# Softmax division moved from VectorE to ScalarE in two attentions

## The chip, the cores and the metric

The kernel runs on one core of one Trainium2 chip. The metric is the device time of one execution in microseconds. The kernel before takes 1680.43 us, the median of three runs (1677.56 to 1681.21 us).

## The reference, cut to what matters

A first model of two layers (gated linear attention, an mLSTM, a mixture of experts after each) is followed by a second one of two layers, called l0 and l1 here. Only the attentions of the second are touched. Each of its layers has two of them, over 256 tokens, with heads of 64 columns:

```python
s = jnp.einsum('bqgrd,bkgd->bgrqk', qi, k) * scale      # attention A: 8 query heads, 2 key heads
p = jax.nn.softmax(s, axis=-1)
o = jnp.einsum('bgrqk,bkgd->bqgrd', p, v)
# attention B: three dilated groups for each of 4 heads; their three softmaxes are
# joined by softmax(lse), which is one softmax over the keys of all three groups
```

A softmax is computed as the row's maximum, the exponential of the shifted scores with the row's sum, the reciprocal of the sum, and a product of each row with its reciprocal. That product is what moves.

In each layer a conditioning vector c also makes six columns of shifts, scales and gates, `silu(c) @ w_ada + b_ada`, from 24 MB of weights. The text calls this the ada work.

## The kernel before, in words

The five engines run their own instruction lists in order and wait for each other by semaphores. The lists are written by a Python program that calls every operation once, in program order, so the list of an engine is the order of the calls. All calls go through a wrapper (`Timed`, L165), so the profile has L175 for nearly every instruction; rows are told apart by their tiles.

**The dense stream.** The kernel multiplies in fp32 by splitting every weight w into hi (ScalarE cast, 128x1024) and lo (VectorE, w minus hi), with three matmuls each (X_H with hi, X_H with lo, X_L with hi). Weights come in units of 1 MB through the SP queue; `Stream.split` (L351) makes hi and lo two chunks ahead of their use. If hi is late, lo is late, because lo reads hi.

**Background work.** Attention, norms and ada work are Python generators, advanced by `B.tick()` after each small group of dense matmuls. So their instructions stand between those of the dense stream, on each engine.

**Two attentions in a layer.** `attend_a` (L2168) runs in four instances, two at a time: scores `sa` (PSUM bank group `acc`, four banks), `softmax` (L2140), transposes of the result `pa` into `pta`, a copy to `pTa`, and the product `oa`. A round is two instances at once: two maxima `mx`, eight exponentials of 128x256, two reciprocals `smx`, eight divisions. While a round runs, its scores hold all four acc banks until the exponentials have read them. The transposes `rtp` of the next queries and keys need such banks. `attend_b` (L2198) runs in four instances as well, with 128x512 tiles `pb`, four exponentials and four divisions in a round.

**What sets the order.** The program keeps a clock of its own (`Clock`, L107, with costs in `Timed.cost`, L187): an estimate of when each engine is through. Three kinds of decisions hang on it. `AV` (L235) puts a copy on ScalarE or VectorE, whichever it expects to be done first; `VG2` does so for VectorE and GpSimd. `calm` (L1950) holds back an ada step while ScalarE or VectorE is expected to run over 0.9 us behind TensorE, for up to ten ticks. `Hooks` (L556) releases the small `part` with `fold` matmuls when both engines are expected to have caught up. So an operation that changes its engine moves others.

**The ada work** (`ada_cols`, L1854) goes in pieces of 512 KB through a ring of two tiles `ada_w`. A piece is a DMA, a ScalarE copy with a scale for each partition into `ada_t`, a VectorE scalar_tensor_tensor that adds its second half, and from the second piece on an addition. Four pieces make a group, which ends in a transpose, a reduction into `part`, and the fold on TensorE. The load of the next piece but one is issued when a piece's VectorE step has read its tile. A layer must have ten groups before its second norm: `emit` (L2306) in the output projection calls `ada_need(l, 9)` (L1957), which issues the remaining pieces with no dense matmuls between them.

Of the kernel before, what the change touches and what calls it, by code (L numbers as in the profile page):

```python
# [30 lines left out]
AF = mybir.ActivationFunctionType  # L31
OP = mybir.AluOpType
# [195 lines left out]
def tile_model(ctx: ExitStack, tc: tile.TileContext, I, out, stages=None, h_in=None):  # L228
    nc = tc.nc
    clock = Clock()  # L230
    PE, V, A, G = [Timed(clock, e, n) for e, n in
                   ((nc.tensor, "PE"), (nc.vector, "V"), (nc.scalar, "A"), (nc.gpsimd, "G"))]
# [1788 lines left out]
    def attention(l, x, at):  # L2021
# [118 lines left out]
        def softmax(pss, held, ps_, ng):  # L2140

            mx = small.tile([P, 2, ng], F32, name="mx", tag="mx", bufs=4)
            for i in range(2):
                V.tensor_reduce(mx[:, i], pss[i], axis=AX.X, op=OP.max)
            V.tensor_scalar(mx, mx, -0.125, None, op0=OP.mult)
            yield 1
            sm = small.tile([P, 2, ng], F32, name="smx", tag="smx", bufs=4)
            for i in range(2):
                for j in range(ng):
                    A.activation(ps_[i][:, j], pss[i][:, j], AF.Exp, bias=mx[:, i, j:j + 1], scale=0.125,  # L2150
                                 accum_out=sm[:, i, j:j + 1])
            for b in held:
                b[0] = True
            yield 1
            V.reciprocal(sm, sm)
            for i in range(2):
                for j in range(ng):
                    V.tensor_scalar(ps_[i][:, j], ps_[i][:, j], sm[:, i, j:j + 1], None, op0=OP.mult)
            yield 1

        oaT = (at.tile([P, 4, T], F32R, name="oaTh"), at.tile([P, 4, T], F32R, name="oaTl"))
# [6 lines left out]
        def attend_a(j):  # L2168
            yield from wait_for(0, 1)
            yield  # L2170
            yield from room(2)
            pss = [acc_ps((P, 2, T), name="sa", read=False) for _ in range(2)]
            held = banks[-2:]
            for mt in range(2):
                for r in range(2):
                    s = slice(r * 64, r * 64 + 64)
                    PE.matmul(pss[r][:, mt], qaT[s, j, mt * P:(mt + 1) * P], kaT[s, 0], start=True, stop=True)
            yield
            pp = [at.tile([P, 2, T], F32, name="pa", tag="p", bufs=4) for _ in range(2)]
            yield from softmax(pss, held, pp, 2)  # L2180
            pT = at.tile([P, 2, 2, T], F32, name="pTa", tag="pT", bufs=2)
            for r in range(2):
                yield from room(1)
                tp = acc_ps((P, 2, 2, P), name="pta")
                for kt in range(2):
                    for mt in range(2):
                        PE.transpose(tp[:, kt, mt], pp[r][:, mt, kt * P:(kt + 1) * P], c_ident)
                AV.copy(pT[:, r], tp.rearrange("p k m q -> p k (m q)"))
                yield
            yield from room(1)  # L2190
            o = acc_ps((P, T), name="oa")
            for kt in range(2):
                for r in range(2):
                    PE.matmul(o[r * 64:r * 64 + 64], va[:, kt, r * 64:r * 64 + 64], pT[:, r, kt],
                              start=kt == 0, stop=kt == 1)
            put_o((oaT[0][:, j], oaT[1][:, j]), o)

        def attend_b(j, mt):  # L2198
# [16 lines left out]
            yield  # L2215
            pp = [at.tile([P, 1, 512], F32, name="pb", tag="p", bufs=4) for _ in range(2)]
            yield from softmax(pss, held, pp, 1)
            pT = at.tile([P, 2, 4, P], F32, name="pTb", tag="pT", bufs=2)
            for r in range(2):
# [450 lines left out]
```

## Time and profile before

| what | number |
|---|---|
| median of three runs | 1680.43 us |
| the profiled execution's own time | 1678.68 us |
| its span (first to last instruction) | 1676.6 us |
| TensorE busy | 1552.8 us |
| VectorE busy | 954.2 us |
| ScalarE busy | 699.6 us |
| attention of l0 in the span | about 884 to 1008 us |
| attention of l1 in the span | about 1306 to 1428 us |
| mean granted TensorE clock | 0.97 |

In the profile PE is TensorE, DVE is VectorE, ACT is ScalarE, POOL is GpSimd and SP is the queue that issues the loads. A row of a timeline has the start in us, the length in us of the instruction or of several alike, the engine, the operation, the tile written and the tiles read, the shape, a count, and in brackets the idle time of the engine just before and what released it.

### The profile page before, as it was taken

To read this page: it belongs to the slowest core of one execution; us is meant where nothing else is said; L and a number is where in the kernel's file an instruction comes from. 1 tells how busy PE (TensorE), PEld (TensorE's weight loads), DVE (VectorE), ACT (ScalarE), POOL (GpSimd) and SP (SyncE) were. 2 spreads that over 40 slices of the span, in tenths; PEclk is the share of its full clock that TensorE was granted. 3 is DMA by queue.
4 is the path that set the end of the run, shared out by engine and by line. 5 is a ranking of instruction groups with operands and counts; after the bars stand their busy time and mean duration, and the time that the engine had idled before them with its cause. 6 is when DMAs were issued, how large, how long until landed. Compare 5 with 4: busy or idle time off the path is not lost. (4 is left out here: it accounts for less than half of the span.)

```text
span 1676.6 us, 22592 instructions
## 1 busy us (share of the span) xinstructions
PE 1552.8 (93%) x8773; PEld 1118.0 (67%) x8774; DVE 954.2 (57%) x1640; ACT 699.6 (42%) x1130; POOL 200.0 (12%) x187
## 2 busy tenths in 40 slices
PE   7998999898899989998889998699998999999996
PEld 5865444336776644443367897589986779879995
DVE  3676113106787531111288868777779976875543
ACT  5533111104544221111155654566565555465552
POOL 1010000001333100000142100200015310020000
PEclk9999999999999999999999999899999999999999
DMA  9847999999765399999854666588875446746551
GB/s 320 302 157 258 351 401 411 393 383 210 254 202 218 119 339 360 406 404 386 300 201 139 201 177 236 155 276 287 286 264 172 151 159 171 237 164 225 177 175 50
DMA packets 165771, 422.44 MB, mean 252 GB/s; under 512 B 13017, under 2 KB 14193, under 8 KB 154642
## 3 DMA queue, kind: packets, MB, share of 16 engines
q1 hardware_dynamic: 165458, 420.75, 72.1%
q8 instruction: 73, 1.20, 0.3%
q14 instruction: 48, 0.39, 0.1%
q0 software_dynamic: 192, 0.10, 0.0%
HBM read 419.77 MB, written 1.05 MB: 251 GB/s over the span
## 5 line engine op out<-in xcount | busy, mean ns | idle before, releaser
L175 DVE TENSOR_TENSOR lo<-w,hi 128x1024 fp32r<-128x1024 f32 x282 | 346.4, 1238 | 131.3 <-ACT hi L175 130.9
L175 ACT CAST hi<-w 128x1024 fp32r<-128x1024 f32 x301 | 310.0, 1051 | 99.8 <-PE mm L175 69.7
L175 PE MATMUL mm<-hi,X_H 128*128 128x512 f32 x512 | 216.2, 422 | 16.2 <-ACT X_H L175 8.5
L175 PE MATMUL mm<-lo,X_H 128*128 128x512 f32 x512 | 207.0, 404 | 3.2 <-DVE lo L175 2.9
L175 PE MATMUL mm<-X_H,hi 128*128 128x256 f32 x704 | 202.8, 288 | 0.0
L175 PE MATMUL mm<-X_L,hi 128*128 128x256 f32 x704 | 199.0, 283 | 0.0
L175 PE MATMUL mm<-X_H,lo 128*128 128x256 f32 x704 | 199.0, 283 | 0.0
L175 PE MATMUL mm<-hi,X_L 128*128 128x512 f32 x512 | 192.8, 399 | 2.5 <-DVE X_L L175 2.4
L175 PE MATMUL up<-w,X 128*64 128x512 f32 x672 | 193.7, 597 | 0.6 <-ACT X L175 0.6
L175 PEld LDWEIGHTS mm<-X_H,hi 128*128 128x128 f32 x704 | 134.5, 191 | 1.7 <-issue 0.7
L175 PEld LDWEIGHTS mm<-X_L,hi 128*128 128x128 f32 x704 | 134.7, 191 | 0.4
L175 PEld LDWEIGHTS mm<-X_H,lo 128*128 128x128 f32 x704 | 134.6, 191 | 0.0
L175 PEld LDWEIGHTS mm<-hi,X_H 128*128 128x128 f32 x512 | 99.3, 194 | 48.6 <-issue 14.1
L175 PEld LDWEIGHTS up<-w,X 128*64 128x64 f32 x672 | 58.6, 137 | 96.4 <-issue 92.8
L175 PEld LDWEIGHTS mm<-lo,X_H 128*128 128x128 f32 x512 | 99.7, 195 | 25.3 <-DVE lo L175 6.6
L175 PEld LDWEIGHTS mm<-hi,X_L 128*128 128x128 f32 x512 | 97.8, 192 | 27.1 <-DVE X_L L175 5.6
L175 PE MATMUL up<-wh,X 128*64 128x512 f32 x336 | 115.9, 601 | 0.0
L175 DVE SCALAR_TENSOR_TENSOR y<-dn,gsl,y 128x512 fp32r<-128x512 f32 x32 | 24.0, 750 | 158.5 <-ACT y L175 158.5
L175 PE MATMUL dn<-w,hTt 128*64 128x512 f32 x336 | 102.8, 614 | 2.1 <-ACT hTt L175 2.1
L175 PE MATMUL acc<-lo,fh 128*128 128x512 f32 x256 | 100.7, 393 | 0.3 <-DVE lo L175 0.3
L175 PE MATMUL acc<-hi,fl 128*128 128x512 f32 x256 | 100.8, 394 | 0.0
L175 PE MATMUL acc<-hi,fh 128*128 128x512 f32 x256 | 99.6, 389 | 0.0
(412 smaller groups left out, 2524.1 us busy)
## 6 DMA issues: line engine op xcount, KB each, us to landing
w<-in_moe_w SPq DMA_DIRECT2D x126, 1024.0 KB, 11.2
w<-in_w_ff SPq DMA_DIRECT2D x64, 1024.0 KB, 5.6
wh<-in_moe_w SPq DMA_DIRECT2D x124, 512.0 KB, 11.5
ada_w<-in_w_ada SPq DMA_DIRECT2D x96, 512.0 KB, 4.9
w<-in_w_in SPq DMA_DIRECT2D x40, 1024.0 KB, 5.4
w<-in_mlstm_w_in SPq DMA_DIRECT2D x16, 1024.0 KB, 19.3
w<-in_gla_w_in SPq DMA_DIRECT2D x12, 1024.0 KB, 9.8
w<-in_w_out SPq DMA_DIRECT2D x8, 1024.0 KB, 5.1
```

Of the source, the lines that this page charges most:

```text
L175: r = f(*args, **kw)
```

## The change

The division of each row of exponentials by its sum is an activation Copy on ScalarE with a scale for each partition, in place of a tensor_scalar on VectorE. The operands and the places of the calls are the same. Over the two layers these are 32 instructions on 128x256 and 16 on 128x512.

```diff
             V.reciprocal(sm, sm)
             for i in range(2):
                 for j in range(ng):
-                    V.tensor_scalar(ps_[i][:, j], ps_[i][:, j], sm[:, i, j:j + 1], None, op0=OP.mult)
+                    A.activation(ps_[i][:, j], ps_[i][:, j], AF.Copy, scale=sm[:, i, j:j + 1])
             yield 1
```

The order of other instructions moves with it. On ScalarE, in the first round of attention A in l0 (hi is the split of a weight, kbT a transposed key, sq a square for a norm, raw a sum of the ada work):

```order
 L175 CAST hi<-w 128x1024
 L175 COPY kbT_11584<-rtp 128x2x128
-L175 COPY raw<-mm 128x4
+L175 ACTIVATE pa<-pa,smx 128x256 x8
 L175 CAST hi<-w 128x1024
 L175 COPY kbT_11584<-rtp 128x2x128
 L175 ACTIVATE sq<-mm 128x256 x2
-L175 COPY pTa<-pta 128x512 x4
+L175 COPY pTa<-pta 128x512 x3
```

The eight divisions now stand ahead of the next hi, and one of the four copies pTa has gone to VectorE. The fold whose sum raw was copied here comes later.

On VectorE, just ahead of the maxima of the second round in l0 (xs, ro and rt are the rotary embedding, ada_t the ada work):

```order
 L175 TENSOR_TENSOR rt<-xs,cs 128x4x32
 L175 TENSOR_TENSOR xs<-ro,rt 128x256
+L175 SCALAR_TENSOR_TENSOR ada_t<-ada_w,ccol,ada_t 128x512
 L175 TENSOR_REDUCE mx<-sa 128x2 x2
 L175 TENSOR_SCALAR mx<-mx 128x4
```

An ada step that stood in the first round, behind the divisions, is now ahead of these maxima. The same move is in l1.

On VectorE, at the end of l0's output projection, around the two residual sums that `emit` makes for the first 128 tokens (res, h):

```order
 L175 TENSOR_TENSOR res<-mm,gt 128x512
 L175 TENSOR_TENSOR h<-h,res 128x512
-L175 STREAM_TRANSPOSE ada_t<-ada_t 128x512
-L175 TENSOR_REDUCE part<-ada_t 128x16
+L175 SCALAR_TENSOR_TENSOR ada_t<-ada_w,ccol,ada_t 128x512
+L175 TENSOR_TENSOR ada_t<-ada_t 128x512
 L175 TENSOR_TENSOR res<-mm,gt 128x512
 L175 TENSOR_TENSOR h<-h,res 128x512
-L175 COPY raw<-bgp 128x4
+L175 SCALAR_TENSOR_TENSOR ada_t<-ada_w,ccol,ada_t 128x512
+L175 TENSOR_TENSOR ada_t<-ada_t 128x512
+L175 STREAM_TRANSPOSE ada_t<-ada_t 128x512
```

At this point the ada work is two pieces further back than it was: they stood in the attention before. On the SP queue the run of ada loads at this place has eight in a row where it had six. Behind it the lists of all engines are the same again until the attention of l1.

## Rows read from the trace of the kernel before

**Rows 1.** The page: span, and busy time by engine.
```profile
span 1676.6 us, 22592 instructions
PE 1552.8 (93%) x8773; PEld 1118.0 (67%) x8774; DVE 954.2 (57%) x1640; ACT 699.6 (42%) x1130; POOL 200.0 (12%) x187
```
**Rows 2.** Busy time by stretch; PEclk is TensorE's granted clock.
```profile
890.00:910.00 20.00, 18.77 (x104) 13.86 (x105) 16.96 (x39) 13.98 (x34) 6.45 (x8) 1.00 0.50 160
910.00:930.00 20.00, 18.10 (x89) 13.16 (x86) 17.14 (x43) 11.39 (x33) 3.73 (x4) 0.91 0.41 131
970.00:990.00 20.00, 20.00 (x166) 18.03 (x165) 11.77 (x18) 11.35 (x22) 0.00 (x0) 1.00 0.73 171
1043.00:1058.00 15.00, 1.83 (x22) 1.23 (x21) 9.73 (x18) 4.41 (x10) 0.00 (x0) 0.65 0.70 228
```
**Rows 3.** Timeline of PE: matmuls behind idle time.
```profile
905.32 0.81 PE L175 MATMUL pta<-ident,pa 128*128 128x128 f32 x4 [0.45 <-DVE pa L175]
...
922.94 0.44 PE L175 MATMUL rtp<-ident,xs 128*128 128x128 f32 x2 [0.72 <-ACT pa L175]
...
1057.35 0.29 PE L175 MATMUL bgp<-part,fold 128*32 128x4 f32 x8 [12.21 <-DVE part L175]
...
1343.56 0.44 PE L175 MATMUL rtp<-ident,xs 128*128 128x128 f32 x2 [1.79 <-ACT pa L175]
```
**Rows 4.** By tile: count, then shortest, median and longest in ns.
```profile
L175 DVE TENSOR_SCALAR pa<-pa,smx x32: 341/348/372, 903.6 to 1354.3; 128x256 f32<-128x256 f32 x32
...
L175 DVE TENSOR_SCALAR pb<-pb,smx x16: 479/484/489, 967.6 to 1421.3; 128x512 f32<-128x512 f32 x16
...
L175 ACT ACTIVATE ada_t<-ada_w,ccol x96: 706/722/770, 57.6 to 1561.6; 128x512 f32<-128x512 f32 x96
```
**Rows 5.** Timeline of ACT, first round of attention A in l0.
```profile
901.18 1.08 ACT L175 CAST hi<-w 128x1024 fp32r<-128x1024 f32 x1
902.12 0.42 ACT L175 COPY kbT<-rtp 128x256 f32<-128x256 f32 x1
...
904.14 0.67 ACT L175 ACTIVATE sq<-mm 128x256 f32<-128x256 f32 x2
...
907.99 1.07 ACT L175 COPY pTa<-pta 128x512 f32<-128x512 f32 x2 [1.23 <-PE pta L175]
908.95 1.06 ACT L175 CAST hi<-w 128x1024 fp32r<-128x1024 f32 x1
...
911.96 0.73 ACT L175 ACTIVATE ada_t<-ada_w,ccol 128x512 f32<-128x512 f32 x1
...
921.86 0.47 ACT L175 ACTIVATE pa<-sa,mx 128x256 f32<-128x256 f32 x1 [7.29 <-DVE mx L175]
```
**Rows 6.** Timeline of DVE, from the first round to the second's maxima.
```profile
903.64 1.14 DVE L175 TENSOR_SCALAR pa<-pa,smx 128x256 f32<-128x256 f32 x4
...
908.15 0.75 DVE L175 SCALAR_TENSOR_TENSOR ada_t<-ada_w,ccol,ada_t 128x512 f32<-128x512 f32 x1
910.04 1.23 DVE L175 TENSOR_TENSOR lo<-w,hi 128x1024 fp32r<-128x1024 f32 x1 [1.14 <-ACT hi L175]
...
920.28 1.28 DVE L175 TENSOR_REDUCE mx<-sa 128x2 f32<-128x512 f32 x2
```
**Rows 7.** Timeline of DVE, end of the output projection of l0.
```profile
1043.41 0.70 DVE L175 STREAM_TRANSPOSE ada_t<-ada_t 128x512 f32<-128x512 f32 x1
...
1047.56 1.42 DVE L175 SCALAR_TENSOR_TENSOR ada_t<-ada_w,ccol,ada_t 128x512 f32<-128x512 f32 x2 [1.13 <-ACT ada_t L175]
...
1052.96 0.75 DVE L175 SCALAR_TENSOR_TENSOR ada_t<-ada_w,ccol,ada_t 128x512 f32<-128x512 f32 x1 [3.26 <-ACT ada_t L175]
...
1054.35 0.75 DVE L175 SCALAR_TENSOR_TENSOR ada_t<-ada_w,ccol,ada_t 128x512 f32<-128x512 f32 x1
```
**Rows 8.** Timeline of ACT, the same place.
```profile
1046.82 1.32 ACT L175 ACTIVATE ada_t<-ada_w,ccol 128x512 f32<-128x512 f32 x2
1052.21 0.72 ACT L175 ACTIVATE ada_t<-ada_w,ccol 128x512 f32<-128x512 f32 x1 [4.07 <-DMA ada_w<-in_w_ada]
```

## The prediction

> **What bounds the kernel now.** I read the page first: TensorE (PE) is busy for 1552.8 of 1676.6 us, VectorE (DVE) for 954.2 and ScalarE (ACT) for 699.6 [rows 1]. So an engine that loses or gains work counts only where PE waits for it, and the average shares say nothing on that. The second view was the busy time by stretch. In attention B PE is busy for 20.00 of 20 us while DVE has 11.77 and ACT 11.35; in attention A PE idles for 1.23 us of one stretch and 1.90 of the next, with the granted clock at 0.91 in the latter; at the end of l0's output projection PE works for 1.83 of 15 us, at a clock of 0.65 [rows 2]. The third was PE's timeline with the brackets that name the releaser: in attention A it waits 0.45 us for the divided `pa`, and then for the exponentials of the next round, 0.72 us in l0 and 1.79 in l1, since the `rtp` transposes need a score bank that those have still to read; at the end of the projection it waits 12.21 us for `part` of the ada work [rows 3]. The tiles gave durations, the timelines of ACT and DVE what stands before each wait.
>
> **Price of the instruction.** On DVE a 128x256 division lasts 348 ns and a 128x512 one 484 [rows 4]. Four in a row take 1.14 us [rows 6], so they start (1.14 - 0.35)/3 = 0.26 apart; for the large ones I take 0.48 less the same overlap of 0.09, 0.40. DVE loses 32 x 0.26 + 16 x 0.40 = about 15 us of queue, ACT gets the same work at its own price. No row shows a 128x256 ACT copy with a scale for each partition. From below: two `sq` of that size, without such a scale, take 0.67 together, 0.28 apart if each lasts 0.39. From above: the 128x256 exponential lasts 0.47 [rows 5], with no overlap 0.5. The nearest row is the same operation at 512 columns, `ada_t`, 0.72 long [rows 4], two in 1.32 [rows 8], 0.60 apart. Two `pTa` of 512 columns take 1.07 [rows 5], 0.48 apart if one lasts 0.59; against `sq` 256 columns less are worth 0.20. I take 0.60 - 0.20 = 0.40 apart: eight take 3.2 us on ACT, 2.4 on DVE with the reciprocal between them.
>
> The Trainium skill prices this too. Its page "ScalarE: Activation LUTs" (section "What ACT_TABLE_LOAD costs") gives 186 ns, 0.833 ns a column, 93 ns for each pointer operand and 93 ns of overlap back to back. That is an estimate of 0.49 us long and 0.40 apart here; at 512 columns it is 0.71, where the trace has 0.72, so the trace agrees and the sum would be the same. The page's section "Rules for kernel authors" says that a multiplication belongs on VectorE and not on ScalarE, which speaks against the change; by the traces so far the larger price bears it out only where ACT is on the chain.
>
> **First round of attention A in l0.** On ACT the divisions come ahead of the next `hi` and of `sq`, `pTa` (order above), and they can't start before the reciprocals, which DVE does just ahead of 903.64 [rows 6]. ACT was through with that round's exponentials by 901.18, then did a `hi` and `kbT` [rows 5]; the other `hi`, which started at about 902.4, now stands behind eight divisions. They run from about 903.7 to 906.9. Behind them come that `hi` with 0.95, `kbT` 0.27, two `sq` 0.55 and three `pTa` about 1.5 (0.48 apart): the `hi` that started at 908.95 [rows 5] starts at about 910.2, 1.2 late. Its `lo`, which DVE began at 910.04 after an idle 1.14 us for `hi` [rows 6], begins at 911.2. DVE works from that `lo` to the maxima at 920.28 [rows 6] almost without a gap, so these are 1.2 late. The ada step that ran at 908.15 in idle time for 0.75 [rows 6] is now in this stretch ahead of the maxima (order above): 0.66 more. The exponentials start at 921.86 after ACT had idled 7.29 us for the maxima [rows 5]; they now start 1.9 later, and PE's `rtp` with them. PE itself gets the transposes of `pa` some 0.9 us later than at 905.32 [rows 3], which is ahead of the same wait and is swallowed by it. l1 shows the same wait for exponentials at 1343.56 [rows 3] and the same moves: 1.9 again.
>
> **Second rounds and attention B.** In the second round of A PE needs six of the eight divided tiles; the dearer ACT price and the copies ahead of them make these 0.3 us late in l0 and, as two copies more stand ahead there, 0.5 in l1. Attention A: 2.2 + 2.4 = 4.6. In attention B 4 x (0.60 - 0.40) = 0.8 us a round is hidden by PE, which has no idle time there while ACT has 8.65 of 20 free [rows 2]: cost 0. Without that cover a round costs up to 4 x 0.60 = 2.4.
>
> **The ada work at the end of l0.** What the attention has not done of it `emit` forces, with no matmuls between. By the order two pieces more are left: eight loads where there were six. Before, two pieces were added at 1047.56, then DVE idled 3.26 us until 1052.96 for a pair whose second step was at 1054.35 [rows 7]; ACT had idled 4.07 for the load [rows 8], whose tile came free only with the first pair. Then the fold ran at 1057.35 [rows 3]. So pair follows pair by 1052.96 - 1047.56 = 5.4 us: add, load, scale. A pair more costs at most that, and at least two DVE steps, 1.4 (two in 1.42 [rows 7]), if its data lies ready. Worked through with those gaps: the first extra step is added from about 1043.4, in the place of the transpose [rows 7], the second from 1047.5, since its load waits for a tile as the one of 1052.96 did; the next two at 1051.4 and 1053.7, the last two at 1057.1 and 1059.3, 4.9 later than 1054.35. I take 4.9, near the row of a full step. All of it is on the path, because PE idles behind it; on SP the next weights stand behind the ada loads and come later by no more than that, which PE doesn't feel while it waits. By the order the lists are then the same again until l1, whose ada work is finished early: no such term there.
>
> **Sum.** 2.2 + 2.4 + 4.9 = 9.5 us on the profiled execution's own 1678.68, 1688.2. That execution lies 1.75 below the median of the runs, 1680.43; so 1689.9 is predicted. From both sides: at 0.28 a division nothing is late on ACT but the ada step, 0.7 a layer, which with 1.4 for the ada pieces gives 2.8, or 1683.2; at 0.50 the eight take 0.8 more in each of the four rounds, 3.2, and with 5.4 at the tail 13.2, or 1693.6.
>
> **Rivals.**
> - *Faster: DVE is relieved where it holds PE.* For: each wait of PE in attention A ends in something DVE works ahead of (the maxima; `pa` itself), and ACT idles 7.29 us before the exponentials [rows 5]. In the 2.4 us that DVE gains it does the following `lo` and norms sooner, and the chain to the maxima shortens by 2.3 if `hi` is not the later one; 2 x 2.3 = 4.6, or 1675.8. It decides if the divisions are through by 905.3, in time for the `hi` behind. Against: DVE already idles 1.14 us for `hi` at 910.04 [rows 6], so its gain would be spent waiting; and the tail's term stays. 0.12.
> - *No change: covered.* The extra ada loads have landed while PE still multiplies, and the tail gives 0 to 1.4; the late exponentials are made up in attention B, as PE's waits of 0.72 and 1.79 [rows 3] come from a bank that frees one tile at a time. 0 to 3, middle 1681.9. Against: a forced run of loads that ACT and DVE already wait for [rows 7, 8]. 0.20.
> - *More: the clock.* Behind its waits PE's granted clock is lower, 0.91 and 0.65 in the two stretches with idle time [rows 2], between the levels of 1.2 and 2.4 GHz. If the longer waits stretch these, the matmuls behind them take twice as long: with 1.9 us of added wait in each layer and 4.9 at the tail I put 2 to 5 on top, about 1693.5. 0.10.
>
> **How the numbers follow.** The forecast has 0.58. A measurement of this kernel can tell 0.2%, 3.4 us, from no change: same is 1677.1 to 1683.8. Slower: 0.58 + 0.10, less 0.02 of the forecast's low end, and as much of the covered case reaches past 3.4; 0.68. Same 0.20, faster 0.12. The range from 1679.5 to 1696 leaves out most of the faster case and the top of the clock's; the forecast's own is 1683 to 1694.
>
> **What would show it.** Right: eight `pa` rows on ACT of about 0.5 us, 0.40 apart, ending near 906.9; the `hi` behind `pTa` near 910.2; the second round's exponentials near 923.7 and PE's bracket at that `rtp` longer; eight ada loads at the projection's end, and a bracket of about 17 us in place of 12.21 before the fold; DVE's busy time down, ACT's up, PE's the same. Wrong: a bracket at the fold near 12 us (the ada term fails), exponentials at or before 921.9 (the round's term), or new idle time of PE in attention B (its cover).

## The result, and the profile after

The changed kernel takes 1691.94 us, the median of five runs (1687.0 to 1693.04), beside 1677.56 for the kernel before on the same chip (five runs, 1677.2 to 1681.21). The ratio is 1.0071, with a 95% interval of 1.0056 to 1.0086: 9.4 to 14.4 us slower. The profiled execution took 1692.57 us. Its page, beside [rows 1]:

```profile
span 1690.4 us, 22594 instructions
PE 1558.4 (92%) x8773; PEld 1123.2 (66%) x8774; DVE 941.9 (56%) x1598; ACT 720.4 (43%) x1175; POOL 197.8 (12%) x184
```

DVE lost 12.3 us of work, ACT gained 20.8, and the span grew by 13.8. The engine that lost work was not the one that held the end. PE's busy time rose by 5.6 us with the same 8773 matmuls.

**Where the time went.** In all kernels told of here VectorE makes the same 282 `lo` in the same order. So the time between the same two of them measures a stretch of the program, whatever else has moved. Eight of them, read from the timeline of VectorE, bound seven stretches (starts in us):

| `lo` at, before | `lo` at, after | what begins there | growth up to the next |
|---|---|---|---|
| 848.91 | 849.36 | start of l0 and its attention A | +2.59 |
| 939.20 | 942.25 | attention B of l0 | +0.02 |
| 1005.28 | 1008.35 | l0's projections | +3.05 |
| 1040.95 | 1047.07 | end of the projection, forced ada work | +5.64 |
| 1072.25 | 1084.01 | the feed-forward half of l0 | -0.30 |
| 1321.85 | 1333.31 | attention A of l1 | +1.93 |
| 1369.00 | 1382.39 | the rest | +0.47 |
| 1653.92 | 1667.78 | | |

The growths sum to 13.4; 0.45 arose ahead of 848.91, in code that the change leaves as it was.

**Attention A.** ACT's timeline, in the columns of [rows 5], and DVE's behind it, to be laid beside [rows 6]:

```profile
904.14 3.30 ACT L175 ACTIVATE pa<-pa,smx 128x256 f32<-128x256 f32 x8 [1.17 <-DVE smx L175]
907.35 1.03 ACT L175 CAST hi<-w 128x1024 fp32r<-128x1024 f32 x1
...
910.51 1.07 ACT L175 CAST hi<-w 128x1024 fp32r<-128x1024 f32 x1
...
924.12 0.47 ACT L175 ACTIVATE pa<-sa,mx 128x256 f32<-128x256 f32 x1 [8.01 <-DVE mx L175]
```
```profile
911.61 1.22 DVE L175 TENSOR_TENSOR lo<-w,hi 128x1024 fp32r<-128x1024 f32 x1 [0.32 <-ACT hi L175]
...
921.85 0.75 DVE L175 SCALAR_TENSOR_TENSOR ada_t<-ada_w,ccol,ada_t 128x512 f32<-128x512 f32 x1
922.51 1.28 DVE L175 TENSOR_REDUCE mx<-sa 128x2 f32<-128x512 f32 x2
```

Eight divisions run in 3.30 us, each 0.49 long: (3.30 - 0.49) / 7 = 0.40 apart. Taking off the 0.45 by which this execution was already late, the `hi` stands at 910.06, its `lo` at 911.16 and the next exponentials at 923.67. That is 1.1, 1.1 and 1.8 later than in [rows 5, 6]. The ada step stands right in front of the maxima.

**TensorE's waits**, in the columns of [rows 3] (`th` is a product with a gate that VectorE makes in the projections):

```profile
925.19 0.55 PE L175 MATMUL rtp<-ident,xs 128*128 128x128 f32 x2 [1.85 <-DVE mx L175]
...
1029.40 0.24 PE L175 MATMUL mm<-part,fold 128*32 128x4 f32 x8 [0.33 <-DVE th L175]
...
1032.00 0.77 PE L175 MATMUL mm<-hi,X_H 128*128 128x512 f32 x1 [2.36 <-DVE th L175]
...
1057.24 0.29 PE L175 MATMUL bgp<-part,fold 128*32 128x4 f32 x8 [5.85 <-DVE part L175]
1069.11 0.29 PE L175 MATMUL bgp<-part,fold 128*32 128x4 f32 x8 [11.59 <-DVE part L175]
```

At `rtp` 0.72 has become 1.85. At l0's end two folds follow one another, with 5.85 + 11.59 = 17.44 us of waiting where there were 12.21 [rows 3]. The waits for `th` of 0.33 and 2.36 were one of 1.60 before, 1.09 less:

```profile
1027.34 0.47 PE L175 MATMUL mm<-hi,X_H 128*128 128x512 f32 x1 [1.60 <-DVE th L175]
```

**Clock.** The busy time by stretch (columns as in [rows 2]) for attention B, and for eight us behind that wait for `th`:

```profile
974.00:994.00 20.00, 20.00 (x166) 18.03 (x165) 13.65 (x20) 11.00 (x21) 0.00 (x0) 1.00 0.68 164
1032.00:1036.00 4.00, 4.00 (x10) 3.17 (x11) 3.93 (x6) 0.17 (x1) 1.28 (x1) 0.50 0.34 133
1036.00:1040.00 4.00, 4.00 (x15) 3.25 (x14) 4.00 (x6) 2.96 (x4) 0.00 (x0) 0.75 0.00 0
```

In attention B TensorE is busy throughout, as before. Behind the wait for `th` it is granted 0.50, the level of 1.2 GHz, for four us and 0.75 over the next four; 10 + 15 = 25 matmuls are counted there. In the kernel before, eight us behind the same wait ran at 1.00, with 39:

```profile
1028.00:1032.00 4.00, 4.00 (x20) 3.27 (x19) 3.97 (x5) 0.90 (x2) 1.29 (x1) 1.00 0.20 75
1032.00:1036.00 4.00, 4.00 (x19) 3.34 (x18) 4.00 (x6) 3.29 (x5) 0.00 (x0) 1.00 0.09 16
```

### The profile page after: what moved, and what is told of

Same layout as the page of the kernel before. It is cut to its first block, busy times and chain, and to the rows that moved or that the text cites. A ratio compares the mean times of both kernels' runs of the same rounds, so it can differ in the third digit from the quotient of the medians.

```text
span 1690.4 us, 22594 instructions
## 1 busy us (share of the span) xinstructions
PE 1558.4 (92%) x8773; PEld 1123.2 (66%) x8774; DVE 941.9 (56%) x1598; ACT 720.4 (43%) x1175; POOL 197.8 (12%) x184
## 4 chain that ended last, share of the span: by engine, by line
PE 28%; DVE 10%; ACT 4%; DMA 4%; issue 3%; POOL 1%; SPq 0%; ACTq 0%; DVEq 0%; POOLq 0%
PE mm L175 18%; PE acc L175 6%; DMA ada_w<-in_w_ada 4%; DVE lo L175 3%; ACT hi L175 2%; DVE ada_t L175 2%; PE sb L175 1%; ACT pa L175 1%; DVE xs L175 1%; DVE h L175 1%; PE tpd L175 1%; DVE hss L175 0%; DVE rt L175 0%; PE ob L175 0%; ACT ada_t L175 0%
```

## The experiments

Each kernel was timed in five rounds beside the kernel before, whose medians were 1678.07 to 1679.14; a gain or loss in us below is the difference from the median beside it. One table sums them up: the ratio with its interval, and from one profile each the growth of the stretches defined above, in us.

| kernel | ratio (95%) | A, l0 | B, l0 | projections | forced ada | A, l1 |
|---|---|---|---|---|---|---|
| changed kernel | 1.0071 (1.0056 to 1.0086) | 2.59 | 0.02 | 3.05 | 5.64 | 1.93 |
| act_old_order | 1.0058 (1.0038 to 1.0077) | 6.39 | -1.07 | 0.03 | -0.03 | 6.31 |
| act_old_raw_v | 1.0027 (1.0012 to 1.0041) | 3.11 | -1.06 | 0.03 | 0.28 | 2.56 |
| dve_new_order | 1.0019 (1.0007 to 1.0031) | 0.12 | 0.00 | 2.17 | 4.51 | 0.99 |
| a_only | 1.0047 (1.0031 to 1.0062) | 2.62 | 0.00 | 3.05 | 4.67 | 0.61 |
| b_only | 1.0038 (1.0025 to 1.0052) | -0.11 | 0.04 | -0.73 | 7.82 | 0.38 |
| second_round_act | 1.0040 (1.0026 to 1.0054) | 0.92 | -0.63 | 2.13 | 7.99 | 0.03 |
| free_hi | 1.0066 (1.0042 to 1.0091) | 2.53 | -0.35 | 3.43 | 4.61 | 1.19 |
| free_hi_ada | 1.0049 (1.0030 to 1.0068) | 2.61 | -0.34 | 0.01 | 8.22 | 0.62 |
| free_ada_dve | 1.0069 (1.0046 to 1.0092) | 8.98 | 3.09 | 6.41 | -8.56 | 2.65 |
| free_ada_act | 1.0113 (1.0083 to 1.0142) | 10.83 | 2.35 | 7.13 | -8.58 | 3.01 |
| b_old_order | 0.9999 (0.9985 to 1.0013) | 0.01 | 0.24 | 0.01 | -0.28 | 0.17 |
| b_old_half_a | 1.0033 (1.0017 to 1.0049) | 3.77 | -0.53 | 0.01 | -0.13 | 3.20 |

The stretch up to 848.91 differed by -4.53 to +2.21 between these profiles, with nothing changed in it; so a single profile's total is worth less than the growths inside it.

The stretch of the forced ada work ends with matmuls behind the last fold, and it is worth parting there. Up to that fold the seven kernels with the changed places of the ada work lost 4.7 to 5.7 us. Behind it b_only, second_round_act and free_hi_ada lost 2.2 to 2.5 more, and the other four nothing. That goes with TensorE's granted clock. In those three it was 0.50 to 0.52 in the second three us behind the fold and 0.61 to 0.68 again at 12 to 15 us; in the other four 0.86 to 0.99, and then 1.00. (act_old_order had 0.54, then 1.00, and lost 0.2 there.) The rows are of the changed kernel, whose fold is at 1069.11, and of free_hi_ada, with the fold at 1066.31:

```profile
1069.11:1072.11 3.00, 3.00 (x15) 2.42 (x16) 1.95 (x8) 1.51 (x3) 1.10 (x1) 0.50 0.29 103
1072.11:1075.11 3.00, 3.00 (x15) 2.45 (x14) 2.40 (x4) 1.05 (x1) 1.33 (x1) 0.99 0.84 226
...
1081.11:1084.11 3.00, 1.96 (x9) 1.26 (x8) 2.90 (x9) 3.00 (x6) 0.00 (x0) 1.00 0.69 197
```
```profile
1066.31:1069.31 3.00, 3.00 (x15) 2.41 (x16) 1.94 (x8) 1.51 (x3) 1.12 (x1) 0.50 0.30 109
1069.31:1072.31 3.00, 3.00 (x9) 2.33 (x8) 1.30 (x3) 1.04 (x1) 1.64 (x1) 0.50 0.81 203
...
1078.31:1081.31 3.00, 1.48 (x4) 1.20 (x5) 2.04 (x7) 2.60 (x8) 0.00 (x0) 0.66 0.64 208
```

**The engine without the order** (act_old_order), and **the order without the engine** (dve_new_order). Edits of the division in `softmax`, with p for the tile and sc for its scale:

```diff
 # act_old_order
-V.tensor_scalar(p, p, sc, None, op0=OP.mult)
+nc.scalar.activation(p, p, AF.Copy, scale=sc)
+clock.run("V", V.cost("tensor_scalar", [p, p, sc], {}), [p], [p, sc])
 # dve_new_order
-A.activation(p, p, AF.Copy, scale=sc)
+nc.vector.tensor_scalar(p, p, sc, None, op0=OP.mult)
+clock.run("A", A.cost("activation", [p, p, sc], {}), [p], [p, sc])
```

> All 48 divisions run on ScalarE, but the program's clock is charged as if they were on VectorE, so every other instruction stands where it stood before. Theory (the ada work displaced by the clock's decisions makes most of the loss; ScalarE's price only a little in attention A): six ada loads forced at l0's end, PE's wait at the fold near 12.2 us, nothing lost in the output projection; what is left is the late hi and the late exponentials in attention A without the ada step ahead of the maxima, +1 to +2 us per layer: +2 to +4 us in all (ratio 1.001 to 1.0025). Rival 1 (ScalarE's price makes it all: its queue is longer, so everything behind is late): +10 to +13 us, as in the changed kernel. Rival 2 (VectorE's relief counts once the order is kept): -2 to -5 us.

> All divisions run on VectorE as before, but the clock is charged as if they were on ScalarE, so every other instruction stands where the changed kernel has it. Theory: eight ada loads forced at l0's end; the tail's 5 to 6 us and the 2 to 3 us in the output projection are there without any division on ScalarE, in attention A the 0.7 us a layer of the ada step ahead of the maxima at most: +7 to +10 us (ratio 1.004 to 1.006). Rival 1 (ScalarE's price makes it all): within 2 us of the kernel before. Rival 2: slower than the changed kernel itself, since VectorE has its divisions back: +13 us or more.

Measured: 1688.32 and 1682.11 us. The order alone, with no division on ScalarE, brings 4.51 of the 5.64 us at l0's end and 2.17 of the 3.05 in the projections, with 0.12 in attention A of l0 and 0.99 in l1; so far the theory holds but for l1, where at most 0.7 was forecast. Its median is +3.5 us, under the 7 forecast. The table's profile is of a run of 1686.61, 4.5 above that median, and so the 6.7 us that it shows in the projections and at l0's end may be less in other runs. The engine alone fell far from the theory: +9.7 us, all in attention A. TensorE's timeline, and ScalarE's ahead of it:

```profile
905.36 0.79 PE L175 MATMUL mm<-hi,X_H 128*128 128x512 f32 x1 [4.97 <-ACT raw L175]
```
```profile
901.97 3.30 ACT L2159 ACTIVATE pa<-pa,smx 128x256 f32<-128x256 f32 x8 [1.17 <-DVE smx L175]
905.17 0.14 ACT L175 COPY raw<-mm 128x4 f32<-128x4 f32 x1
```

`raw` reads a PSUM bank that the next dense matmul needs. In the old order it stands behind eight divisions, and TensorE waits 4.97 us for a copy of 0.14. In the changed kernel the fold, and `raw` with it, comes later and this wait is not there. The reordering costs time at l0's end, and saves some in attention A.

**Only the copy moved** (act_old_raw_v): as act_old_order, with `raw` on VectorE.

```diff
-AV.copy(raw, ps[:, 0:4])
+nc.vector.tensor_copy(raw, ps[:, 0:4])     # first fold behind the round; clock as before
```

> As act_old_order (all divisions on ScalarE, every other instruction in its old place), but the 128x4 copy raw that stands behind the eight divisions of the first round on ScalarE is made on VectorE, in l0 and l1. Theory (in the old order raw holds a PSUM bank that TensorE's next matmul needs, and its 4.97 us wait for raw is what made attention A cost 6.4 us a layer there; the changed kernel escapes it since its fold comes later): attention A falls to +2 to +3.5 us a layer, the end of l0 stays as before, +4 to +7 us in all (ratio 1.0025 to 1.004). Rival (the divisions themselves are what TensorE waits for at its transposes, and raw only stands in the same place): +8 to +11 us, as act_old_order.

Measured: 1683.61 us, +5.5, as the theory had it. One copy in each layer gave back 3.28 and 3.75 us of attention A. What is left, 3.11 and 2.56, has these brackets in l0 and at the end:

```profile
904.92 0.50 PE L175 MATMUL mm<-hi,X_H 128*128 128x512 f32 x1 [1.68 <-DVE raw L1941]
925.74 0.44 PE L175 MATMUL rtp<-ident,xs 128*128 128x128 f32 x2 [0.93 <-DVE mx L175]
...
1060.96 0.29 PE L175 MATMUL bgp<-part,fold 128*32 128x4 f32 x8 [12.61 <-DVE part L175]
```

The last is the old one fold with its old wait: ScalarE's price alone does not touch l0's end.

**One attention at a time** (a_only, b_only). The division is chosen by the count of blocks, `ng == 2` in attention A and `ng == 1` in B, and the program's clock is told the truth.

```diff
+if ng == 2:      # a_only; ng == 1 in b_only
+    A.activation(p, p, AF.Copy, scale=sc)
+else:
     V.tensor_scalar(p, p, sc, None, op0=OP.mult)
```

> Only attention A divides on ScalarE, attention B on VectorE as before; the clock is told the truth. By its order there are eight forced ada loads again. Theory: attention A's 2 to 3 us a layer, and the whole tail: +10 to +13 us (ratio 1.006 to 1.008). Rival (A's divisions cost only their price; the displaced ada work is B's doing): +4 to +5 us.

> Only attention B divides on ScalarE, attention A on VectorE as before; the clock is told the truth. By its order there are eight forced ada loads too. Theory: no loss in attention A and none in B, where TensorE never idles, but the tail and the output projection by the displaced ada work: +5 to +8 us (ratio 1.003 to 1.005). Rival (B's divisions lie beside busy matmuls and cost nothing at all): within 2 us of the kernel before.

Measured: 1686.65 and 1684.70 us, +8.0 and +6.0. Attention A's divisions cost 2.62 us in l0, as in the changed kernel, and 0.61 in l1. Attention B's cost nothing in either attention, and yet there are 7 us more in the projections and at l0's end together, 2.2 of them behind the last fold: the program's clock puts two ada pieces off in either case. b_only's +6.0 is in the range of its theory. a_only's +8.0 lies below the 10 forecast. Its profile can't say why: its stretches from 848.91 on grew by 11.45 us, and the stretch ahead of them was 4.53 shorter.

Why do attention A's divisions cost 1.93 us in l1 of the changed kernel and 0.61 here? Counted from the `lo` that opens the stretch, the second round's `rtp` is 0.74 later than in the kernel before in both, with the same wait of 1.86. VectorE's `lo` behind the late `hi` is 1.13 late in the changed kernel and the ada step adds 0.66, but a pair of `rt` ahead of the maxima that took 1.56 us before takes 0.48:

```profile
1334.64 1.56 DVE L175 TENSOR_TENSOR rt<-xs,cs 128x128 f32<-128x128 f32 x2
```
```profile
1347.23 0.48 DVE L175 TENSOR_TENSOR rt<-xs,cs 128x128 f32<-128x128 f32 x2
```

What parts the two kernels comes behind that `rtp`, and is the clock. In a_only its low stretch began while TensorE waited for exponentials; in the changed kernel it fell on busy matmuls. First come that `rtp` and the ten us from it on in the changed kernel (columns as in [rows 3] and [rows 2]), then the same in a_only:

```profile
1355.76 0.44 PE L175 MATMUL rtp<-ident,xs 128*128 128x128 f32 x2 [1.86 <-DVE mx L175]
```
```profile
1355.70:1360.00 4.30, 1.78 (x9) 0.84 (x9) 2.01 (x5) 4.30 (x17) 0.00 (x0) 0.87 0.54 151
1360.00:1366.00 6.00, 6.00 (x23) 5.42 (x24) 1.64 (x5) 1.61 (x5) 1.01 (x1) 0.52 0.27 104
```
```profile
1350.18 0.44 PE L175 MATMUL rtp<-ident,xs 128*128 128x128 f32 x2 [1.86 <-DVE mx L175]
```
```profile
1350.12:1354.42 4.30, 2.52 (x9) 1.09 (x9) 2.01 (x5) 4.30 (x17) 0.00 (x0) 0.54 0.48 143
1354.42:1360.42 6.00, 6.00 (x28) 5.39 (x29) 1.64 (x5) 2.80 (x8) 1.01 (x1) 0.76 0.28 107
```

**Which round** (second_round_act): the first round of attention A divided on VectorE, in the changed order.

```diff
-A.activation(p, p, AF.Copy, scale=sc)
+nc.vector.tensor_scalar(p, p, sc, None, op0=OP.mult)     # first round; clock as for ScalarE
```

> The changed kernel's order with the first round of attention A, in both layers, divided on VectorE again (the clock charged as for ScalarE), the second round of A and all of B on ScalarE. Theory (of the 2.6 and 1.9 us that attention A loses, the first round's divisions ahead of hi make nearly all, the second round 0.3 to 0.5): attention A costs 0.3 to 0.8 us in l0 and 0.5 to 1.3 in l1, the projection and the tail keep their 7 to 8.5 us: +6 to +10 us against the kernel before (ratio 1.0035 to 1.006). Rival (each round costs its own price of four divisions more): attention A keeps half, 1.3 us in l0, or more.

Measured: 1685.64 us, +6.5, as forecast; attention A 0.92 in l0, a little over the 0.8 of the theory, and 0.03 in l1, under its 0.5, and TensorE's bracket at `rtp` is back to about its old size:

```profile
919.84 0.44 PE L175 MATMUL rtp<-ident,xs 128*128 128x128 f32 x2 [0.90 <-ACT pa L175]
```

So in l0 the first round makes most of attention A's loss, 1.67 of 2.59. That it does so through the late `hi` fits the chain read above; no run moved that `hi` alone.

**The projections** (free_hi, then free_hi_ada). In the changed kernel ScalarE, and VectorE behind it, stood like this ahead of TensorE's wait at 1032.00:

```profile
1021.34 0.60 ACT L175 ACTIVATE gt<-adar 128x512 f32<-128x512 f32 x1 [2.35 <-PE adar L175]
1023.64 0.60 ACT L175 ACTIVATE gt<-adar 128x512 f32<-128x512 f32 x1 [1.71 <-PE adar L175]
1024.68 0.72 ACT L175 ACTIVATE ada_t<-ada_w,ccol 128x512 f32<-128x512 f32 x1 [0.44 <-DMA ada_w<-in_w_ada]
1025.31 1.99 ACT L175 CAST hi<-w 128x1024 fp32r<-128x1024 f32 x2
```
```profile
1026.39 2.36 DVE L175 TENSOR_TENSOR lo<-w,hi 128x1024 fp32r<-128x1024 f32 x2 [2.14 <-ACT hi L175]
1028.66 0.68 DVE L175 SCALAR_TENSOR_TENSOR th<-th,mm 128x512 f32<-128x512 f32 x1
```

```diff
 # both: the one ada copy behind the gates
-A.activation(t, w[:, 0], AF.Copy, scale=ccol[:, 2 * q:2 * q + 1])
+nc.gpsimd.tensor_scalar(t, w[:, 0], ccol[:, 2 * q:2 * q + 1], None, op0=OP.mult)
 # free_hi only: both gates gt of l0's attention
-A.activation(row_b, ps, AF.Copy, scale=scale)
+nc.vector.tensor_scalar(row_b, ps, scale, None, op0=OP.mult)
```

> The changed kernel, but in the output projection of l0 the two copies gt run on VectorE and the one ada copy behind them on GpSimd, so that the two hi behind these on ScalarE wait for TensorE alone; everything else keeps its place. Theory (the output projection lost 3.05 us because these hi started 2 us late, the residual work on VectorE with them, and TensorE's longer wait for th dropped its clock to the lower level): the hi pair starts about 2 us sooner against the lo before it, TensorE's bracket for th goes from 2.36 to 1.2 to 1.8 us, the half-clock stretch behind it shrinks or goes, the projection costs 0 to 1.5 us; the tail keeps its 5 us; 1.5 to 3 us less than the changed kernel, +8 to +11 us against the kernel before (ratio 1.005 to 1.0065). Rival (the projection is slower for another reason, as the second fold that now stands in it): no change against the changed kernel.

> The changed kernel with one instruction moved: the ada copy that stands on ScalarE between the gates gt and the last pair of hi in l0's output projection runs on GpSimd; gt stays on ScalarE, since in free_hi the gates on VectorE waited for adar there and held back the same lo pair. Theory (the projection's 3.05 us come from that late hi pair by way of lo and th on VectorE): hi starts 1.1 us sooner, TensorE's bracket for th falls from 2.36 to about 1.3 us, the clock's low stretch behind it is shorter; the projection costs 0.5 to 2.3 us instead of 3.05, 0.7 to 2.5 us less than the changed kernel. Rival (the second fold, or VectorE's own queue, holds TensorE there): the bracket stays at 2.2 to 2.4 us and the region at about 3 us.

free_hi was inconclusive: 1690.27 us, +11.7, above the 11 forecast. Its `hi` came early, at 1022.70, but the gates on VectorE now waited for `adar` in front of the same `lo`, and TensorE's bracket stayed at 2.36:

```profile
1023.71 0.69 DVE L1982 TENSOR_SCALAR gt<-adar 128x512 f32<-128x512 f32 x1 [1.02 <-PE adar L175]
...
1026.85 2.36 DVE L175 TENSOR_TENSOR lo<-w,hi 128x1024 fp32r<-128x1024 f32 x2
```

free_hi_ada moved the ada copy alone. TensorE's timeline and the busy time of the same four us:

```profile
1031.01 0.47 PE L175 MATMUL mm<-hi,X_H 128*128 128x512 f32 x1 [1.58 <-DVE th L175]
...
1054.52 0.29 PE L175 MATMUL bgp<-part,fold 128*32 128x4 f32 x8 [6.91 <-DVE part L175]
1066.31 0.29 PE L175 MATMUL bgp<-part,fold 128*32 128x4 f32 x8 [11.50 <-DVE part L175]
```
```profile
1032.00:1036.00 4.00, 4.00 (x19) 3.30 (x18) 3.97 (x6) 1.15 (x2) 1.30 (x1) 1.00 0.07 26
```

Counted from the `lo` that opens the projections (1008.54 here), the `hi` came 1.2 us sooner than in the changed kernel, the bracket went back to 1.58, the clock stayed at 1.00, and the projections' growth fell from 3.05 to 0.01, below the 0.5 of the theory. So one copy of 0.72 us that waited 0.44 for its load cost 3 us of the projections. The kernel took 1688.79 us, +9.7; its interval of 1.0030 to 1.0068 overlaps the changed kernel's, so its times alone don't show a gain. In the profile the forced ada work grew by 8.22 instead of 5.64, and that isn't the chain of loads: up to the last fold the stretch grew by 5.69, as in the changed kernel, although TensorE waits longer, 6.91 + 11.50 = 18.41 us, and the fold comes 3.0 us sooner after the start of the projections. The other 2.5 us arose behind the fold, where the clock stayed at 0.50 for six us and fell once more (rows above).

**No forced ada work** (free_ada_dve from the kernel before, free_ada_act from the changed one):

```diff
-            if t <= clock.t["PE"] + 0.9:
+            if t <= clock.t["PE"] + 3.0:
```

> The kernel before, divisions on VectorE, with one number changed: an ada step is held back only while its engine is expected to run over 3 us behind TensorE, not 0.9. By its order the ada work is through in time and no run of forced ada loads is left at l0's end. Theory (the forced pieces there set the tail, some 2.6 us each): TensorE's wait of 12.21 us before the fold falls to under 4 us, the tail gains 6 to 9 us; the ada steps that now stand in the attentions cost 2 to 6 us there; -1 to -6 us in all. Rival (the ada steps are as dear in the attention as at the end, where they are late): 0 to +5 us.

> The changed kernel, divisions on ScalarE, with the same number 3 in place of 0.9; no run of forced ada loads is left either. Theory: the 5.6 us of the tail and the 12 us wait are gone as in free_ada_dve, attention A keeps its 2 to 3 us a layer, and perhaps one us more as the ada copies stand on the fuller ScalarE: +3 to +6 us against free_ada_dve, -3 to +5 us against the kernel before. Rival (ScalarE's fuller queue makes the loss everywhere): +8 us or more against the kernel before.

Measured: 1691.52 and 1698.20 us. The stretch at l0's end gained 8.6 us, as the theory has it, and the folds' wait is gone. The attentions and projections lost 21 and 23, far over the 2 to 6 forecast; the first kernel's rival was right in sign, and short too. free_ada_act's +20.1 fell in its rival's range, but not for the rival's reason: free_ada_dve lost nearly as much in the same places without a division on ScalarE. ScalarE of free_ada_dve shows why, in attention A and in the projections:

```profile
900.75 0.72 ACT L175 ACTIVATE ada_t<-ada_w,ccol 128x512 f32<-128x512 f32 x1 [3.90 <-DMA ada_w<-in_w_ada]
901.38 1.03 ACT L175 CAST hi<-w 128x1024 fp32r<-128x1024 f32 x1
...
1030.94 0.72 ACT L175 ACTIVATE ada_t<-ada_w,ccol 128x512 f32<-128x512 f32 x1 [3.71 <-DMA ada_w<-in_w_ada]
1031.58 1.98 ACT L175 CAST hi<-w 128x1024 fp32r<-128x1024 f32 x2
```

An ada copy that stands there before its load has landed holds the `hi` behind it.

**In search of a better one** (b_old_order, b_old_half_a): attention B on ScalarE with the old order, and then half of attention A too, with `raw` on VectorE.

```diff
+if ng == 1:              # b_old_order; in b_old_half_a: ng == 1 or i == 0
+    nc.scalar.activation(p, p, AF.Copy, scale=sc)
+    clock.run("V", V.cost("tensor_scalar", [p, p, sc], {}), [p], [p, sc])
+else:
     V.tensor_scalar(p, p, sc, None, op0=OP.mult)
```

> The sixteen 128x512 divisions of attention B on ScalarE, attention A's on VectorE, and the clock charged as if all were on VectorE, so that every other instruction keeps the place it had. Theory (attention B is bound by TensorE and the tail's ada work isn't displaced): within 2 us of the kernel before, rather below by the 1 us that this region gained in act_old_order: -2 to +0.5 us. Rival (b_only's 6 us were ScalarE's price after all): +4 to +7 us.

> As b_old_order, and half of attention A's divisions, the first four of each eight, on ScalarE too, the copy raw behind them in the first round on VectorE; all other places as before. Theory: both engines divide at once, the last pa is there some 0.8 us sooner than before, and hi starts at about the time that its lo has room on VectorE, so that attention A costs -1 to +0.5 us a layer: -3 to +1 us in all. Rival (any division ahead of hi on ScalarE is on the path): +1 to +1.5 us a layer, +1 to +3 us.

Measured: 1678.49 us for b_old_order, no change (0.9985 to 1.0013): attention B's divisions on ScalarE cost nothing that can be told once they move nothing else. b_old_half_a took 1685.20 us, +6.6, worse than either forecast. TensorE waited at the same bank once more, because `raw` stood behind VectorE's four divisions there:

```profile
905.96 0.79 PE L175 MATMUL mm<-hi,X_H 128*128 128x512 f32 x1 [3.02 <-DVE raw L1941]
```

Whether half the divisions ahead of `hi` are on the path this run doesn't tell. No kernel beat the one before.

## Why the prediction was right, and where it was not

- **Direction and size.** 1689.9 was forecast, 1691.94 measured, inside the range; +9.5 forecast, 9.4 to 14.4 measured, 14.4 between the medians. That the time came within some 2 us is in part luck: the forecast started from 1680.43, and beside the changed kernel the kernel before took 1677.56. In growth the sum was 3.9 us short of the profile's 13.4.
- **The instruction's price** held: 0.40 us apart, as taken between 0.28 and 0.50. The estimate from the Trainium skill's page "ScalarE: Activation LUTs" (section "What ACT_TABLE_LOAD costs"), 0.49 long and 0.40 apart, agrees with the trace as well.
- **Attention A of l0**: 2.2 forecast, 2.59 measured; `hi` at 910.2 against 910.06, exponentials at 923.7 against 923.67 once the earlier 0.45 is taken off. second_round_act confirms that the first round carries most of it. That the ada step ahead of the maxima costs 0.66 by itself is not shown: the same order with divisions on VectorE lost only 0.12.
- **Attention A of l1**: 2.4 forecast; 1.93 in the changed kernel, but 0.61 to 1.19 in a_only, free_hi and free_hi_ada, which divide on ScalarE there as well. The step over-counted: 0.74 later at the `rtp` where 1.9 was forecast, since a pair of `rt` became 1.08 shorter there, for a cause that isn't shown. That 2.4 came near 1.93 is luck; the rest of the 1.93 came behind that `rtp`, by the clock, and differs from kernel to kernel.
- **Attention B**: 0 forecast, 0.02 measured; b_old_order shows the cover holds.
- **The forced ada work**: 4.9 forecast, 5.64 measured, with eight loads and 17.44 us of waiting where about 17 were expected. act_old_order, act_old_raw_v and b_old_order, with the old order, have 0.3 us or less there; seven kernels with the changed places of the ada work have 4.5 to 8.2, and 4.7 to 5.7 up to the last fold. The term holds, 0.7 short.
- **The step that was missed** is in "All of it is on the path ...": its tacit other half, that nothing is lost ahead of the tail. The ada pieces and gates that left the attention came into l0's projections, in front of a `hi`, and cost 3.05 us there, a term that the sum put at nothing. Against free_hi_ada, which lost 0.01 there, 1.2 us had been lost by the end of the wait for `th` (1032.00 - 1008.35 against 1031.01 - 1008.54), and the other 1.9 from there to the `lo` that ends the stretch (1047.07, against 1044.22), with the clock at its lower level. Together with the forced ada work it makes 8.7 us where 4.9 were forecast.
- **The rival of the clock** was right in kind. It put 2 to 5 us on top of the sum, behind the waits of attention A and of the tail. The clock did cost some 1.9 us, but behind the wait for `th`, and about 1.3 more of attention A in l1 than in a_only; behind the last fold, where it was expected, the changed kernel lost nothing more than the kernel before (14.9 us from the fold to the `lo` that ends the stretch in both). PE's busy time was to stay the same and rose by 5.6 us. The measured time lies between the forecast and this rival's 1693.5.
- **What made up for it**: attention A of l1 0.5 less, the feed-forward half of l0 0.3 less.
- **The faster rival** fell. DVE's 12.3 us of relief bought nothing where the order was kept (act_old_raw_v, b_old_order). The rival that the change is covered holds for attention B alone.
- **Not foreseen at all**: the reordering's good side. I had counted it as a loss only; with the old order the change costs 6.3 to 6.4 us in each attention A, of which `raw` behind the divisions makes 3.3 to 3.7.

## What to carry to other kernels

Where a program places work by its own estimate of engine times, a moved instruction has two prices, its own and that of the order it brings; charge the estimate for the old engine and run the new one, and the other way round, and both can be read apart. On an engine that works in order, look at what stands behind the moved instructions and ask who waits for that: TensorE waited 4.97 us for a copy of 0.14 us behind eight divisions, and 3.3 us came back with that copy elsewhere. And where a wait of TensorE grows, read its granted clock behind the wait: in l0's projections 1.2 us of lateness brought 1.9 more.

## What the runs showed of the hardware beyond what was expected

In the projections, the kernels whose TensorE waited 2.35 or 2.36 us for `th` (the changed kernel, dve_new_order, a_only, second_round_act, free_hi) all had a granted clock below 1.00 behind it, 0.50 over four us in the changed kernel. So had free_ada_dve, 0.64 over three us. But free_ada_act, with 2.36 us for `th` as well, kept 1.00 over the nine us from 1040 on. Those with 1.38 to 1.61 (the kernel before, b_only, free_hi_ada and the ones with the old order) kept 1.00 in front of the same matmuls. From the start of the first to the start of the last of the 72 matmuls behind that wait it took 16.21 us in the kernel before (1027.34 to 1043.55) and 19.00 in the changed kernel (1032.00 to 1051.00).

The length of a wait didn't settle what came behind it. After waits of 11.59 us (the changed kernel) and 11.50 (free_hi_ada) for the last fold the clock stayed at 0.50 for three us and for six. After 1.86 us at the same `rtp` of l1 it was 0.87 over 4.3 us and then 0.52 over six in the changed kernel, and 0.54 and then 0.76 in a_only. What decides in these cases no run here shows.
